# Key stage of a hybrid decoder step: triangles of two pairs inverted together, one running sum in place of two running products, affine steps moved or folded, low-rank products on whole rows

## The chip, the cores and the metric

The kernel runs on one core of a Trainium2 chip. The metric is the device time of one launch, in microseconds (us). Its engines are TensorE (PE in the rows, its weight loads PEld), VectorE (DVE), ScalarE (ACT), GpSimd (POOL) and SyncE (SP, which only issues transfers); each works through its own queue in order.

## The reference

One step of a decoder trunk of two layers: an RWKV-7 layer, then a latent attention layer, for a prompt of 1024 tokens and eight single tokens (the "sample"), in float32. The change lies in the first layer, in what stands ahead of its recurrence:

```python
def _wkv_step(S, inp):
    r, w, k, v, a, b = inp
    sa = jnp.einsum('bhvk,bhk->bhv', S, a)
    S = S * w[:, :, None, :] + sa[..., None] * b[:, :, None, :] + v[..., None] * k[:, :, None, :]
    return S, jnp.einsum('bhvk,bhk->bhv', S, r)
...
    w_log = -jax.nn.softplus(-(w0 + jnp.tanh(xw @ w1) @ w2)) - 0.5
    decay = jnp.exp(-jnp.exp(w_log.astype(F32)))
    a = jax.nn.sigmoid(a0 + (xa @ a1) @ a2)
    kk = heads(k * k_k).astype(F32)
    kk = kk / jnp.maximum(jnp.sqrt(jnp.sum(kk * kk, axis=-1, keepdims=True)), 1e-12)
    k = k * (1 + (a - 1) * k_a)
    xs = (seq(rh), seq(heads(decay)), seq(kh), seq(vh), seq(-kk), seq(kk * ah.astype(F32)))
```

## The kernel before, in words

The recurrence is done in 32 chunks of 32 tokens. What a chunk needs is made ahead, in the key stage, for 16 tiles of 128 channels (two heads each; `ct` is the tile). With `R` the receptance, `K` the key, `TW` and `TA` the hyperbolic tangents from the low-rank products of decay and rate, each tile does this, in the order of the loop over `ct`:

- `score` and `rows` of the tile before (`p`): TensorE forms the scores of a chunk in PSUM (`sc`), VectorE masks them to `XS`, ScalarE copies their triangles to `nts`, which SP stores to the scratch `n_d`; TensorE turns rows (`tr`), ScalarE copies them to `XS`, SP stores `xs_d`.
- `norm`: TensorE sums squares (`ss`), VectorE takes the maximum with a small number (`RN`), ScalarE a logarithm and an exponential of it (lines 784 and 785, a table load before each).
- `newkey`: VectorE makes `GG`, the new key, from `TA` and `K`, and an affine form of `TA`.
- `decay` (at the end of the tile before) and `decay2`: the decay's running product over a chunk, `Wp`, and its inverse, `Wi`, two scans on VectorE.
- `raw_rows`, `unit`, `unit2`, `unit_rows`: `RA` and `BK`, the operands of `score`, on VectorE; POOL multiplies `R` and `GG` into `K` (line 821), from which TensorE later adds up the bonus (`bo`).
- Beside this TensorE does the key projection of the next tile (`kproj`, product `p`, 24 steps a tile) and the two low-rank products (`ua`, product `u`), whose weights are cut in a high and a low part by `lora` and `lcut`.

Of every second tile on, POOL inverts the triangles of two pairs of heads (`inverse`, called by `whole`): (1 - N)^-1 of 128 triangles of 32 x 32, one a partition, in 31 steps, each a product into `Xt` and an addition to `X` (lines 1081 and 1083). Step s has (s+1) x (31-s) elements a partition. The triangles come back from `n_d` as `N`, and the result goes to `u_d`. The generator of the steps is `pend[0]`: `steps(g, n)` issues n steps of the projection and, after three of each four, one of the inverse. So the engines' queues are written by the order of the program: what POOL does for a tile stands behind the inverse steps that were issued before. The eighth inverse runs on VectorE at the end (`iv7`). The line that decides the pace:

```python
            def steps(g, n):
                for u in range(n):
                    next(g, None)
                    if u % 4 != 3:
                        next(pend[0], None)
```

A float32 product of the projections is made of three products of rounded parts (`mm3`, all on line 62). All pools give their buffers in turn, and an instruction waits for the reader of the buffer that it takes.

Of the kernel before, what the change touches and what calls it, by code (L numbers as in the profile page):

```python
# [11 lines left out]
F32 = mybir.dt.float32  # L12
F32R = mybir.dt.float32r
# [8 lines left out]
P = 128  # L22
# [22 lines left out]
# columns of the host-made constant table  # L45
# [10 lines left out]
def tile_yoco(ctx, tc, A, O, dbg=None):  # L56
    """A: name -> DRAM AP of the inputs, O: list of the ten DRAM outputs."""
# [36 lines left out]
    u_d = scr("u_d", (NC, 4, C, 6, C))  # L94
    u2_d = scr("u2_d", (NC, 2, 4, C, C))
# [2678 lines left out]
```

## Time and profile before

| | |
|---|---|
| time, median of 3 runs | 3003.13 us (2996.41 to 3007.01) |
| profiled execution, span | 3038.3 us, on the one core; granted TensorE clock 0.956 on the mean |
| TensorE busy | 2773.3 us, 91% of the span |
| VectorE, ScalarE, POOL busy | 1684.0, 1360.0, 1425.9 us |
| key stage, first `ss` of tile 0 to the last store of an inverse | 462.3 to 1004.2 us |

The span is that of the profiled execution, from its first to its last instruction; a time of its own beside the span is not given. Busy times are unions of an engine's instructions. An engine that is idle costs nothing by itself; what counts is which wait ends last.

### The profile page before, as it was taken

To read this page: it belongs to the slowest core of one execution; us is meant where nothing else is said; L and a number is where in the kernel's file an instruction comes from. 1 tells how busy PE (TensorE), PEld (TensorE's weight loads), DVE (VectorE), ACT (ScalarE), POOL (GpSimd) and SP (SyncE) were. 2 spreads that over 40 slices of the span, in tenths; PEclk is the share of its full clock that TensorE was granted. 3 is DMA by queue.
4 is the path that set the end of the run, shared out by engine and by line. 5 is a ranking of instruction groups with operands and counts; after the bars stand their busy time and mean duration, and the time that the engine had idled before them with its cause. 6 is when DMAs were issued, how large, how long until landed. Compare 5 with 4: busy or idle time off the path is not lost.

```text
span 3038.3 us, 64866 instructions
## 1 busy us (share of the span) xinstructions
PE 2773.3 (91%) x26386; PEld 2416.2 (80%) x26386; DVE 1684.0 (55%) x2952; ACT 1360.0 (45%) x2886; POOL 1425.9 (47%) x1385
## 2 busy tenths in 40 slices
PE   7999999878778788888789999999999999699998
PEld 7999997666567677777689899988888888465897
DVE  7233128979788466765752441176766666333424
ACT  7232127767656354445543452144444444233323
POOL 3222121899999366751354463123333332555342
PEclk9999999989889899999899999999999999899999
DMA  4332335667569899999675533231111111656535
GB/s 152 133 112 72 101 87 129 171 148 175 144 150 237 200 225 220 215 232 207 193 225 165 151 89 102 70 96 50 50 51 50 50 48 36 196 195 200 174 96 183
DMA packets 567501, 423.80 MB, mean 139 GB/s; under 512 B 176260, under 2 KB 515649, under 8 KB 567074
## 3 DMA queue, kind: packets, MB, share of 16 engines
q1 hardware_dynamic: 473954, 336.06, 41.2%
q10 hardware_dynamic: 79648, 38.42, 4.8%
q0 software_dynamic: 13600, 45.16, 4.7%
q8 instruction: 208, 3.41, 0.5%
q14 instruction: 91, 0.75, 0.1%
HBM read 281.69 MB, written 133.35 MB: 137 GB/s over the span
## 4 chain that ended last, share of the span: by engine, by line
PE 58%; DVE 7%; POOL 6%; DMA 5%; issue 4%; ACT 3%; SPq 1%; ACTq 0%; another core or an unknown queue 0%; DVEq 0%; POOLq 0%
PE sc L62 8%; PE p L62 7%; PE zb L62 6%; PE bo L62 5%; PE wop L62 4%; PE o L62 4%; POOL X L1083 2%; POOL Xt L1081 2%; PE q L62 2%; PE pt L2157 2%; PE s L62 2%; PE pt L2576 2%; PE k L62 2%; PE v L62 2%; PE ssc L62 1%
## 5 line engine op out<-in xcount | busy, mean ns | idle before, releaser
L76 POOL TENSOR_TENSOR wl<-wr,wh 128x1024 fp32r<-128x1024 f32 x32 | 84.2, 2653 | 287.5 <-ACT wh L71 269.8
L1081 POOL TENSOR_TENSOR Xt<-N,X 128x31 f32<-128x31 f32 (+15 forms) x217 | 188.7, 870 | 26.5 <-DMA N<-n_d 10.4
L1083 POOL TENSOR_TENSOR X<-X,Xt 128x31 f32<-128x31 f32 (+15 forms) x217 | 182.1, 839 | 17.0
L71 ACT CAST pth<-pt 128x256 fp32r<-128x256 f32 (+1 forms) x320 | 108.1, 354 | 139.8 <-DVE ptl L76 70.6
L1289 DVE TENSOR_TENSOR st<-s,gC 64x512 f32<-64x512 f32 x128 | 88.2, 689 | 130.0 <-PE s L62 127.5
L62 PE MATMUL p<-mh,w3h 128*128 128x344 f32 x384 | 149.1, 388 | 7.8 <-issue 6.6
L76 DVE TENSOR_TENSOR ptl<-pt,pth 128x256 fp32r<-128x256 f32 (+1 forms) x320 | 121.1, 392 | 29.1 <-ACT pth L71 27.0
L62 PE MATMUL p<-mh,w1h 128*128 128x344 f32 x360 | 136.0, 378 | 0.0
L62 PE MATMUL p<-ml,w3h 128*128 128x344 f32 x384 | 130.0, 339 | 2.2 <-DVE ml L76 2.2
L62 PE MATMUL p<-mh,w3l 128*128 128x344 f32 x384 | 126.8, 336 | 2.1 <-issue 2.1
L62 PE MATMUL r<-mh,wh 128*128 128x344 f32 x384 | 124.2, 323 | 3.3 <-ACT tf L483 3.1
L62 PE MATMUL r<-mh,wl 128*128 128x344 f32 x384 | 123.8, 323 | 0.0
L62 PE MATMUL r<-ml,wh 128*128 128x344 f32 x384 | 123.7, 322 | 0.0
L62 PE MATMUL p<-ml,w1h 128*128 128x344 f32 x360 | 120.7, 335 | 0.0
L62 PE MATMUL p<-mh,w1l 128*128 128x344 f32 x360 | 120.5, 335 | 0.0
L2509 POOL DMA_INDIRECT pg<-in_cache_ckv_dram,idx x64 | 60.6, 947 | 100.9 <-issue 50.8
L2140 ACT ACTIVATE pr<-sc,mx 128x128 f32<-128x128 f32 (+7 forms) x128 | 95.4, 745 | 26.7 <-DVE mx L2137 22.8
L2041 POOL TENSOR_TENSOR qp<-qp,rope 128x256 f32<-128x256 f32 (+1 forms) x30 | 22.2, 740 | 172.1 <-DMA qsw<-qp 167.3
L2137 DVE TENSOR_REDUCE mx<-sc 128x1 f32<-128x128 f32 (+7 forms) x128 | 96.8, 756 | 3.2
L1305 ACT COPY y<-y 32x256 f32<-32x256 f32 x256 | 93.0, 363 | 11.3 <-PE y L62 7.7
L62 PEld LDWEIGHTS s<-st,xz 128*64 128x64 f32 x2048 | 72.8, 148 | 30.1 <-issue 22.0
L1950 DVE TENSOR_TENSOR zbr<-zb,RS 128x384 f32<-128x384 f32 (+1 forms) x48 | 24.6, 515 | 127.4 <-PE zb L62 125.2
(1237 smaller groups left out, 9971.4 us busy)
## 6 DMA issues: line engine op xcount, KB each, us to landing
xs_d<-XS SPq DMA_DIRECT2D x64, 512.0 KB
xz<-xs_d SPq DMA_DIRECT2D x64, 512.0 KB
wr<-in_a_w_in_dram SPq DMA_DIRECT2D x17, 1024.0 KB
ra_d<-RA SPq DMA_DIRECT2D x32, 512.0 KB
xz<-ra_d ACTq DMA_DIRECT2D x58, 256.0 KB
rT_d<-rr ACTq DMA_DIRECT2D x16, 516.0 KB
R<-rT_d SPq DMA_DIRECT2D x16, 516.0 KB
w3r<-in_a_w_in_dram SPq DMA_DIRECT2D x16, 512.0 KB
```

What stands on the lines that cost most here:

```text
L62: PE.matmul(out, lhsT=lhsT, rhs=rhs, start=start, stop=stop)
L71: ACT.copy(out, in_)
L76: (eng or V).tensor_tensor(out, in_, hi_.bitcast(F32), ALU.subtract)
L1081: eng.tensor_tensor(t3, N_[:, s_:s_ + 1, s_ + 1:].to_broadcast([P, a, b]), X_[:, r0:r1, s_:s_ + 1].to_broadcast([P, a, b]), ALU.mult)
L1083: eng.tensor_tensor(X_[:, r0:r1, s_ + 1:], X_[:, r0:r1, s_ + 1:], t3, ALU.add)
L1289: V.tensor_tensor(ST[s_][1 - c % 2][rows, qs, :], p3[rows], gC[rows, qs, c:c + 1].to_broadcast([64, 8, 64]), ALU.mult)
L1305: ACT.copy(ys[B][ts(ci, 32), a:a + 2].rearrange("p a s d -> p (a s d)"), p_[ts(j, 32), 0:256])
L2137: V.tensor_reduce(mx, sc[:, :W], AX.X, ALU.max, negate=True)
L2140: ACT.activation(pr[:, :W], sc[:, :W], AF.Exp, bias=mx, accum_out=sm)
L2157: PE.transpose(pt[:, ts(q, P)], pr[:, ts(g + q, P)], ident)
L2509: G.indirect_dma_start(t_.rearrange("p r c -> p (r c)"), None, A[nm].rearrange("n (q r) c -> (n q) (r c)", r=4), off)
L2576: PE.transpose(p_[:, ts(r, P)], pg[:, r, ts(c, P)], ident)
```

## The change

It has four parts, all in the key stage.

1. `inverse` takes a list of one or two inverses and does their steps in the same instructions, over [128, 2, rows, columns]. `GROUPS` starts inverse 0 alone in tile 2, and the pairs 1 and 2, 3 and 4, 5 and 6 in tiles 6, 10 and 14. `pace` says after which of four projection steps an inverse step is issued: three of four for a single one and for the last pair, one of four for the others. Inverse 5 now goes to the second scratch `u2_d`, with 6 and 7.
2. The decay's running products become one running sum `CS` of `TW` + 1 (added on POOL), with one scan on VectorE whose factor `E0` (one byte) is zero at the head of a chunk. `Wp`, `Wi` and the chunk's end `gC` are then exponentials of it on ScalarE.
3. `GG`'s affine step goes to ScalarE. `TA`'s is folded into the products that read it.
4. The low-rank weights stand in both halves of the partitions, so that both products of `ua` and the cuts in `lcut` go over 128 rows. Some buffers have one copy in place of two.

```diff
             def lora(ct):
+                raw = kp.tile([P, 2, P], F32, tag="l2r", name=f"l2r{ct}")
+                for u in range(2):
+                    SY.dma_start(raw[ts(u, 64), 0], A["a_w2"][0][:, ts(ct, P)])
+                    SY.dma_start(raw[ts(u, 64), 1], A["a_a2"][0][:, ts(ct, P)])
...
-                        mm(p_[:, :NQ], d["l2"][me], th2[i][me, nsl[n]], False, True)
+                        mm(p_[:, :NQ], d["l2"][:, i], th2[i][:, nsl[n]], False, True)
...
             def decay(ct):
-                ACT.activation(Wp[:, :, 1:33], c3(TW), AF.Exp, bias=cneg, scale=-0.5 * CDEC)
-                ACT.activation(Wi[:, :, 1:33], c3(TW), AF.Exp, bias=cpos, scale=0.5 * CDEC)
+                G.tensor_scalar(CS[:, :, 1:33], c3(TW), 1.0, None, ALU.add)
...
             def decay2(ct):
-                for t_ in (Wp, Wi):
-                    V.memset(t_[:, :, 0:1], 0.0)
-                V.tensor_tensor_scan(fl(Wp), fl(Wp), fl(E0), 0.0, ALU.mult, ALU.add)
-                V.tensor_tensor_scan(fl(Wi), fl(Wi), fl(E0), 0.0, ALU.mult, ALU.add)
-                V.tensor_copy(gC[:, ct, :], Wp[:, :, 32])
+                V.tensor_tensor_scan(fl(CS), fl(E0), fl(CS), 0.0, ALU.mult, ALU.add)
+                ACT.activation(fl(Wp), fl(CS), AF.Exp, scale=-0.5 * CDEC)
+                ACT.activation(Wi, CS[:, :, 1:33], AF.Exp, scale=0.5 * CDEC)
+                ACT.activation(gC[:, ct, :], CS[:, :, 32], AF.Exp, scale=-0.5 * CDEC)
...
-                V.tensor_scalar(GG, TA, dv[:, 2, ct:ct + 1], dv[:, 3, ct:ct + 1], ALU.mult, ALU.add)
-                V.tensor_scalar(TA, TA, -0.5, -0.5, ALU.mult, ALU.add)
+                ACT.activation(GG, TA, AF.Identity, bias=dv[:, 3, ct:ct + 1], scale=dv[:, 2, ct:ct + 1])
...
-                V.tensor_tensor(d["TA"], d["TA"], d["RN"], ALU.mult)
+                V.scalar_tensor_tensor(d["TA"], d["TA"], 1.0, d["RN"], ALU.add, ALU.mult)
...
-                    if u % 4 != 3:
+                    if u % 4 in pace[0]:
                         next(pend[0], None)
...
+            GROUPS = {2: [0], 6: [1, 2], 10: [3, 4], 14: [5, 6]}
+            pace = [(0, 1, 2)]
+
+            def whole(qs):
+                n, q = len(qs), qs[0]
+                bufs = [ivp.tile([P, 2, C * C], F32, tag=t_, name=f"{t_}{q}")[:, 0:n] for t_ in "NX"]
+                pace[0] = (0, 1, 2) if n == 1 or q == 5 else (0,)
+                return inverse(qs, (*bufs, ivp.tile([P, C * C // 2], F32, tag="Xt", name=f"Xt{q}")), G, late)
...
         for s_ in range(C - 1):
+            a, b = s_ + 1, C - 1 - s_
+            t4 = tm[:, :n * a * b].rearrange("p (n a b) -> p n a b", n=n, b=b)
+            eng.tensor_tensor(t4, N_[:, :, s_:s_ + 1, s_ + 1:].to_broadcast([P, n, a, b]),
+                              X_[:, :, 0:a, s_:s_ + 1].to_broadcast([P, n, a, b]), ALU.mult)
+            eng.tensor_tensor(X_[:, :, 0:a, s_ + 1:], X_[:, :, 0:a, s_ + 1:], t4, ALU.add)
             yield
```

TensorE keeps its order. On POOL, in the changed kernel, this stands at the end of tile 6 and in tile 7 (the last of the first eight double steps, `CS` of tile 7, three double steps, and the product into tile 7's `K`; the numbers in the names tell buffers apart):

```order
L1081 TENSOR_TENSOR Xt_6229<-N_6227,X_6228 128x384
L1083 TENSOR_TENSOR X_6228<-X_6228,Xt_6229 128x2x8x24
L789 TENSOR_SCALAR CS<-TW_6271 128x32x32
L1081 TENSOR_TENSOR Xt_6229<-N_6227,X_6228 128x414
L1083 TENSOR_TENSOR X_6228<-X_6228,Xt_6229 128x2x9x23
L1081 TENSOR_TENSOR Xt_6229<-N_6227,X_6228 128x440
L1083 TENSOR_TENSOR X_6228<-X_6228,Xt_6229 128x2x10x22
L1081 TENSOR_TENSOR Xt_6229<-N_6227,X_6228 128x462
L1083 TENSOR_TENSOR X_6228<-X_6228,Xt_6229 128x2x11x21
L818 TENSOR_TENSOR K_6025<-R_6263,GG_6405 128x1024
```

Before, at the product into `K` of such a tile, POOL had this:

```order
L1081 TENSOR_TENSOR Xt_6338<-N_6336,X_6337 128x255
L1083 TENSOR_TENSOR X_6337<-X_6337,Xt_6338 128x17x15
L821 TENSOR_TENSOR K_6128<-R_6371,GG_6517 128x1024
L1081 TENSOR_TENSOR Xt_6338<-N_6336,X_6337 128x252
L1083 TENSOR_TENSOR X_6337<-X_6337,Xt_6338 128x18x14
```

A new instruction, `CS`, stands behind the steps of a tile; `K` stood behind 17 steps of its inverse there and stands behind three of the next tile's twelve now.

VectorE at the head of tile 7, before:

```order
L783 TENSOR_SCALAR RN_6505<-ss_2_6512 128x344
L806 TENSOR_SCALAR GG_6517<-TA_6380,dv 128x1032
L807 TENSOR_SCALAR TA_6380<-TA_6380 128x1032
L808 TENSOR_TENSOR GG_6517<-GG_6517,K_6128 128x1032
L796 MEMSET Wp 128x32
L796 MEMSET Wi 128x32
L797 SCALAR_TENSOR_TENSOR Wp<-Wp,E_4223 128x1056
L798 SCALAR_TENSOR_TENSOR Wi<-Wi,E_4223 128x1056
L799 COPY gC<-Wp 128x32
L813 TENSOR_TENSOR BK<-GG_6517,Wi 128x16x32
```

The same place of the changed kernel (the scans are printed as instructions of two tensors and a scalar):

```order
L782 TENSOR_SCALAR RN_6393<-ss_2_6400 128x344
L805 TENSOR_TENSOR GG_6405<-GG_6405,K_6025 128x1032
L794 SCALAR_TENSOR_TENSOR CS<-E_4224,CS 128x1056
L810 TENSOR_TENSOR BK<-GG_6405,Wi 128x16x32
```

Three instructions are left between `RN` and `BK` where there were nine, of which `GG` has an operand from ScalarE, the scan one from POOL and `BK` one from ScalarE.

ScalarE at the same place, of the changed kernel (before, `Wp` and `Wi` stood ahead of the logarithm, and the copies of `tr` came right behind the exponential of line 785):

```order
L783 ACT_TABLE_LOAD
L783 ACTIVATE RN_6393<-RN_6393 128x1032
L784 ACT_TABLE_LOAD
L784 ACTIVATE RN_6393<-RN_6393 128x1032
L804 ACTIVATE GG_6405<-TA_6272,dv 128x1032
L795 ACTIVATE Wp<-CS 128x1056
L796 ACTIVATE Wi<-CS 128x1024
L797 ACTIVATE gC<-CS 128x32
L870 COPY XS_0_6351<-tr_0_6433 64x4x64
```

`GG` has come in, and the two large exponentials and `gC` stand between it and the copies, behind VectorE's scan.

## Rows read from the trace of the kernel before

**Rows 1.** Windows by tiles: stretch, length, busy time (and count) of each engine, clock, DMA

```profile
core 0: us, PE busy (x) PEld busy (x) DVE busy (x) ACT busy (x) POOL busy (x), PEclk, DMA share, GB/s
462.30:512.80 50.50, 47.04 (x397) 38.44 (x396) 46.05 (x72) 38.41 (x72) 5.52 (x2) 0.94 0.44 108
512.80:563.10 50.30, 49.25 (x489) 40.17 (x485) 47.49 (x67) 42.54 (x87) 24.49 (x26) 1.00 0.77 187
563.10:626.00 62.90, 52.59 (x486) 42.53 (x484) 58.12 (x73) 43.01 (x87) 58.29 (x64) 0.89 0.65 155
626.00:756.90 130.90, 104.52 (x972) 84.92 (x968) 111.99 (x142) 86.24 (x173) 120.63 (x135) 0.90 0.67 158
756.90:886.40 129.50, 104.58 (x974) 85.02 (x969) 111.39 (x141) 86.07 (x173) 119.28 (x133) 0.89 0.67 157
886.40:927.80 41.40, 27.06 (x244) 22.05 (x242) 26.68 (x34) 21.23 (x42) 38.30 (x44) 0.79 0.55 138
```

**Rows 2.** Waits of TensorE, 462 to 928: sum, times, longest

```profile
PE bo L62 <- POOL K L821: 52.0, 9, 13.7
```

**Rows 3.** Timeline of POOL, tiles 3 to 5: start, length, instruction, idle before

```profile
540.54 0.24 POOL L1081 TENSOR_TENSOR Xt<-N,X 128x31 f32<-128x31 f32 x1 [9.26 <-DMA N<-n_d]
540.86 0.25 POOL L1083 TENSOR_TENSOR X<-X,Xt 128x31 f32<-128x31 f32 x1
...
544.33 2.41 POOL L1081 TENSOR_TENSOR Xt<-N,X 128x112 f32<-128x112 f32 x1
...
601.20 2.35 POOL L821 TENSOR_TENSOR K<-R,GG 128x1024 f32<-128x1024 f32 x1
...
605.17 0.65 POOL L1081 TENSOR_TENSOR Xt<-N,X 128x31 f32<-128x31 f32 x1
```

**Rows 4.** Timeline of POOL in the recurrence, two instructions of 512 elements

```profile
1040.23 1.04 POOL L1169 TENSOR_TENSOR tm<-sa,vs 128x512 f32<-128x512 f32 x1
1041.35 1.26 POOL L1171 TENSOR_TENSOR S<-S,tm 128x512 f32<-128x512 f32 x1
```

**Rows 5.** Timeline of VectorE, heads of tiles 1 and 2

```profile
490.96 0.81 DVE L806 TENSOR_SCALAR GG<-TA,dv 128x1032 f32<-128x1032 f32 x1
491.80 0.70 DVE L807 TENSOR_SCALAR TA<-TA 128x1032 f32<-128x1032 f32 x1
492.41 1.23 DVE L808 TENSOR_TENSOR GG<-GG,K 128x1032 f32<-128x1032 f32 x1
...
493.81 2.36 DVE L797 TENSOR_TENSOR_SCAN Wp<-Wp,E 128x1056 f32<-128x1056 f32 x1
...
498.52 0.69 DVE L813 TENSOR_TENSOR BK<-GG,Wi 128x512 f32<-128x512 f32 x1
...
518.92 2.36 DVE L797 TENSOR_TENSOR_SCAN Wp<-Wp,E 128x1056 f32<-128x1056 f32 x1
```

**Rows 6.** Timeline of ScalarE, head of tile 1: logarithm and exponential

```profile
491.49 1.07 ACT L784 ACTIVATE RN<-RN 128x1032 f32<-128x1032 f32 x1
...
493.87 1.07 ACT L785 ACTIVATE RN<-RN 128x1032 f32<-128x1032 f32 x1
```

**Rows 7.** Line 2049 on POOL, one input: least, median and greatest length in ns

```profile
L2049 POOL TENSOR_SCALAR qp<-qp x30: 847/849/1268, 1992.5 to 2537.5; 128x256 f32<-128x256 f32 x30
```

**Rows 8.** Groups by line, 455 to 970: busy, mean ns, idle before, releasers

```profile
L62 PEld LDWEIGHTS u<-th,l2l 64*128 64x128 f32 x96 | 18.2, 189 | 21.3 <-issue 21.0 <-DVE l2l L76 0.3
```

**Rows 9.** Chain of waits, tile 2: start, length, what

```profile
531.80 8.60 DMA N<-n_d
```

**Rows 10.** Timeline of POOL at the stage's end: stores of the last inverses

```profile
992.03 2.01 POOL L1091 DMA_DIRECT2D u_d<-X  x4 [0.29 <-POOL X L1083]
1002.71 1.93 POOL L1091 DMA_DIRECT2D u_d<-X  x4 [8.67 <-DVE X L1083]
```

**Rows 11.** Timeline of VectorE in the last inverse, two additions of 112 elements

```profile
975.21 0.73 DVE L1083 TENSOR_TENSOR X<-X,Xt 128x112 f32<-128x112 f32 x1
...
1000.56 0.27 DVE L1083 TENSOR_TENSOR X<-X,Xt 128x112 f32<-128x112 f32 x1
```

More of the change, by code (lines that the diff above doesn't have):

```diff
@@ L219, in phase_a @@
             omx = hp.tile([P, 48], F32, name="omx")
+            shT = hp.tile([P, KT, NB], F32, name="shT")
             w1x = px.enter_context(ExitStack())
@@ L619, in phase_a @@
             Wp = kp.tile([P, NC, 33], F32, name="Wp")
-            Wi = kp.tile([P, NC, 33], F32, name="Wi")
-            E0 = kp.tile([P, NC, 33], BF16, name="E0")
+            Wi = kp.tile([P, NC, 32], F32, name="Wi")
+            CS = kp.tile([P, NC, 33], F32, name="CS")
+            E0 = kp.tile([P, NC, 33], mybir.dt.uint8, name="E0")
             rkb = kp.tile([P, KI, H], F32, name="rkb")
@@ L670, in lcut @@
                 raw = st[ct]["l2r"]
-                s2 = st[ct]["s2"] = [kp.tile([P, P], F32R, tag=f"l2h{i}", name=f"l2h{i}_{ct}", bufs=2) for i in range(2)]
-                l2 = st[ct]["l2"] = kp.tile([P, P], F32R, tag="l2l", name=f"l2l{ct}", bufs=2)
-                for i in range(2):
-                    me = slice(64 * i, 64 * i + 64)
-                    hi(s2[i][0:64], raw[me])
-                    hi(s2[i][64:128], raw[me], V)
-                    lo(l2[me], raw[me], s2[i][me])
+                s2 = st[ct]["s2"] = kp.tile([P, 2, P], F32R, tag="l2h", name=f"l2h{ct}")
+                l2 = st[ct]["l2"] = kp.tile([P, 2, P], F32R, tag="l2l", name=f"l2l{ct}")
+                hi(s2, raw)
+                lo(l2, raw, s2)
             def rload(ct):
@@ L765, in evac @@
                         if ct == n == 0:
-                            zbank[1] = kp.tile([P, T], F32, tag="GG", name="zrow0", bufs=2)
+                            zbank[1] = kp.tile([P, T], F32, tag="GG", name="zrow0")
                         ACT.copy(zbank[1][:, nsl[n]], p_)
@@ L914, in phase_a @@
             zg = chain(*(zproj(ct, ct == 0) for ct in range(KI)))
-            def whole(q):
-                bufs = [ivp.tile([P, C * C], F32, tag=t_, name=f"{t_}{q}", bufs=b_) for t_, b_ in (("N", 2), ("X", 2))]
-                return inverse(q, (*bufs, [ivp.tile([P, C * C // 4], F32, tag="Xt", name=f"Xt{q}")]), [(G, 0, C)], late)
+            GROUPS = {2: [0], 6: [1, 2], 10: [3, 4], 14: [5, 6]}
[5 more added lines that the diff above has]
+                return inverse(qs, (*bufs, ivp.tile([P, C * C // 2], F32, tag="Xt", name=f"Xt{q}")), G, late)
             for ct in range(KI - 1):
@@ L953, in phase_a @@
                     rows(p, 3)
-                if ct % 2 == 0 and p >= 0:
+                if ct in GROUPS:
                     run(pend[0])
-                    fresh = whole(p // 2)
+                    fresh = whole(GROUPS[ct])
                     next(fresh)
@@ L971, in phase_a @@
                     mz_cut(1, G, G)
-                if ct % 2 == 0 and p >= 0:
+                if ct in GROUPS:
                     pend[0] = fresh
@@ L980, in phase_a @@
                 decay(ct + 1)
-                if ct == KI - 2:
-                    late.pop(0)()
+            assert not late
             p, ct = KI - 2, KI - 1
@@ L1021, in phase_a @@
             ra_store(ct, 0)
-            ivb.append([kp.tile([P, 16, C], F32, tag="nts", name="Xt7").rearrange("p a b -> p (a b)")])
-            iv7 = inverse(KI // 2 - 1, ivb, [(V, 0, C)], late)
+            ivb.append(kp.tile([P, 16, C], F32, tag="nts", name="Xt7").rearrange("p a b -> p (a b)"))
+            iv7 = inverse([KI // 2 - 1], ivb, V, late)
             next(iv7)
@@ L1037, in phase_a @@
             late[1]()
-            bT = kp.tile([H, T], F32, tag="GG", name="bT", bufs=2)
+            bT = kp.tile([H, T], F32, tag="TA", name="bT", bufs=2)
             for i in range(4):
```

67 lines of the change are left out of this document (29 added, 38 removed).

## The prediction

> **What bounds the kernel now.** I read the trace from the outside in. First the busy time of each engine between the first norm products (`ss`) of chosen tiles, which cuts the key stage into stretches that the changed kernel has too [rows 1]. Tiles 2 and 3 take 25.2 us each (50.30 / 2), with TensorE busy 24.6 us a tile, VectorE 23.7, ScalarE 21.3: nothing is spare and TensorE is the nearest to a bound. From tile 4 on it is another picture: 62.9 us for two tiles, 130.9 and 129.5 for four, 41.4 for the last, and in all of these POOL is busy more than nine tenths. Then the waits of TensorE: its longest sum is `bo` for POOL's `K` (line 821), 52.0 us [rows 2]. Then POOL's own rows in order of time [rows 3]: one inverse of a pair of heads starts at 540.54 and the next at 605.17, so POOL gives out one in 64.6 us, two tiles, and `K` stands in its queue between the steps. So POOL sets the pace of tiles 4 to 14, through the place of `K` in its queue, and the other engines set 25 us where POOL is free.
>
> **What a POOL instruction costs.** Alone, 31 elements take 0.24 us as a product and 0.25 as an addition [rows 3], 512 elements 1.04 and 1.26 [rows 4]; that is 0.19 us fixed, plus 1.66 ns and 2.10 ns an element, and about 0.08 between two. One inverse is 31 steps of (s+1)(31-s) elements, 5456 in all: 62 x 0.27 + 5456 x 3.76 ns = 37.2 us. With two `K` of 2.35 that makes 41.9; the period is 64.6. The other 22.7 us, 11 a tile, come from VectorE: a product of 112 elements, 0.38 by this rule, takes 2.41 us when it meets a scan [rows 3], 2.0 more.
>
> **The change part by part.**
> *Pairs.* 62 instructions of double size do two inverses: 62 x 0.27 + 10912 x 3.76 ns = 57.7 us instead of 74.4. Three times this saves 17 us of POOL, but see where the steps stand. A tile issues 20 steps of a single inverse, but 12 of a double one.
> *One scan.* VectorE loses 2.36 us and POOL some 2.0 us of obstruction a tile; two exponentials move behind the scan, `gC` moves to ScalarE. A scan over bytes instead of BF16 is not in the trace; the two scans there bound it (2.36 for the first, no reason for a gain).
> *Affine steps.* `GG` (0.81) and `TA` (0.70) leave VectorE [rows 5]; `GG` comes on ScalarE, 1.07 as the neighbours of the same 1032 elements [rows 6], and behind both of them. The -0.5 and the +1 go into instructions that exist; as three-operand forms I leave them at their old time. The +1 of the decay becomes a POOL instruction of 1024 elements (`CS`). Between 2.35 (`K`, same size, two inputs) and four times the one-input row of 256 elements, 0.849 [rows 7], less three fixed parts: 2.8. I take 2.8, the same operation. The Trainium skill, GPSIMD Engine Reference, section Engine selection, says that one-input work on GpSimd runs at roughly line rate; that would make `CS` an estimated 1.1 us and the total 14 us less. Rows 7 disagree: 0.849 for 256 elements is slower than a two-input sum of the slope above.
> *Whole rows.* The 96 half-height products leave; 21.0 us of idle time stood before their weights [rows 8]. It is TensorE time, some 1.3 us a tile or more, and TensorE stops being the bound below, so I count nothing; if ScalarE's chain were not there, it would be a gain of up to 20 us. Two more small loads a tile on SP lie ahead of `n_d` by a tile and cost nothing.
>
> **A tile without inverse steps.** At 491.49 ScalarE begins the logarithm, the exponential ends at 494.94 [rows 6]. Before, VectorE meanwhile did `GG`, `TA`, `GG*K` and began the first scan at 493.81, and `BK` came at 498.52 [rows 5]. Now: `GG` on ScalarE to 496.0, `GG*K` (1.23) to 497.3, the scan (2.36) to 499.6, `Wp` and `Wi` (1.07 each by their size) and `gC` to about 502: `BK` 3.3 us later. ScalarE's busy time of 21.3 gets 1.1 for `GG`, 0.2 for `gC`, less 0.2 for the merged casts, and it now stands still 3.6 us from 496.0 to 499.6 for VectorE, with about 1 us of its waits for TensorE left: 27 us a tile against 25.2. VectorE has 23.7 of work, less 3.9 and some small casts and copies, and waits for ScalarE before `GG*K` (some 4.7) and before `BK` (2.3): under 27, hidden behind ScalarE.
>
> **A tile with inverse steps.** `CS` of the next tile is issued at the end of a tile, so in POOL's queue it stands behind every step of that tile; VectorE's scan waits for it, and behind the scan on VectorE stand `BK`, `RA`, the score copies `XS` and everything else, behind `Wp` on ScalarE the transposed rows. Before, `K` stood half a tile ahead of its reader; `CS` has almost no lead. A tile is then POOL's sum from `CS` to `CS`, with VectorE's obstruction at 11 - 2.0 - 0.6 (affine, casts), say 8. A stretch is named by its tiles, from scan to scan, and set against rows 1.
> - 2 to 3: the load of `N` was issued 12.9 us after the scan (518.92 to 531.80) [rows 5, 9]; the rows that go ahead of it begin 3.5 later on ScalarE, of which I keep half, so 14.7. It lands 8.6 later [rows 9], at 23.3. Eight steps of 948 elements 7.9, obstruction 0.6, `CS` 2.9: 34.7.
> - 3 to 4: 20 steps, 4330 elements, 27.1; `K` 2.4, `CS` 2.9, 8: 40.4. Together 75.1 against 50.3: +24.8.
> - 4 to 6, three small steps only: 54 against 62.9: -8.9. 0 to 2: 54 against 50.5: +3.5.
> - 6 to 7: second load 1.8, so 25.1; eight double steps (1896) 11.4, 0.6, 2.9: 40.0. 7 to 8: twelve (5804) 28.3, 2.4, 2.9, 8: 41.6. 8 to 9: eleven (3212) 18.0, 2.4, 2.9, 8: 31.3; VectorE, held longer by longer POOL instructions, needs about 33, taken. 9 to 10: 27. Together 141.6 against 130.9 (+10.7) and against 129.5 for 10 to 14 (+12.1).
> - 14 to 15: 40 and 2.5 for the two cuts of mixed inputs that stand ahead on POOL: 42.5 against 41.4, +1.1.
> - Tail: 23 double steps are 46.3 alone instead of 29.4, +17; `K` of tile 15 no longer stands behind eight steps, -8; POOL had stored its part at 992.03 and been idle 8.67 before the last stores [rows 10], so alone it would just fit. But the last inverse is on VectorE, and beside POOL an addition of 112 elements takes 0.73, afterwards 0.27 [rows 11]: one instruction for each of POOL's. It began near 970, eight instructions before 975.21. With POOL's at 1.1 us on the mean and busy to about 1001 on the old scale, some 29 of the 62 are done by then, and 33 more of 0.2 to 0.43 take 11 us: 1012 against 1002.71. +9. By the Trainium skill, SBUF — State Buffer, section SBUF: two separate sides, the two engines' shared port pair is held by one for a whole instruction and the other fully blocks; the trace agrees in these two rows, and the rule speaks against longer POOL instructions.
>
> Sum: 3.5 + 24.8 - 8.9 + 10.7 + 12.1 + 1.1 + 9 = +52 us. The profiled span of 3038.3 would become 3090; it lies 35 us above the median of the runs shown, whose cause no row shows, and I carry the difference over unscaled: 3003 + 52 = 3055.
>
> **The rivals.**
> *Faster: POOL's total decides, not the order in its queue.* Four tiles then need 57.7 + 4 x 2.4 + 4 x 2.9 + 4 x 8 = 111 us of POOL instead of 130: -38 for both groups, -2 for the first six tiles, -13 for 14 to 15, +9 in the tail: -44, 2959. For it: POOL is the bound of before and its sum falls. Against: the place of `CS`. It decides where VectorE comes to its scan later than POOL to the end of `CS`, that is if VectorE's own tile is over 40 us. I give it and its halves 0.23.
> *No change.* `CS` 2.35 (-4), half the obstruction (-20), a free tile of 25 (-12), a tail of +2 (-7): +9. Small terms must all go one way: 0.09.
> *Slower still.* Instructions over four dimensions 20% dearer an element, which no row shows: +7 in each group, +7 in the tail, and VectorE held as much longer: 3077 to 3090. 0.13.
> The forecast, +15 to +75 by these pieces, has 0.55.
>
> **Numbers.** Within 0.3% (9 us) is about what a measurement of this kernel cannot tell from no change. Slower 0.68, same 0.09, faster 0.23. The range goes down into the halves of the faster rival, where a part of the waits is hidden, and up to the last rival: 2972 to 3088. The forecast's own range is 3018 to 3080.
>
> **What the changed profile would show.** VectorE's scan waits for POOL's `CS`, 10 us or more in tiles 3, 4, 7, 8, 11, 12 and 15; `bo` no longer waits for `K`. `GG*K` waits some 4 us for ScalarE in every tile, `BK` some 2. Tiles 4, 5, 9 and 13 take about 27 us with POOL mostly idle. POOL's largest steps take 1.0 to 1.3 us alone, `CS` near 2.8. The last inverse on VectorE ends later. I am wrong if the scan does not wait for `CS`, if `CS` is near 1 us, or if steps of 512 elements cost hardly more than those of 256.

## The result, and the profile after

The changed kernel takes 3071.7 us (median of 4 runs, 3067.43 to 3078.25), the kernel before on the same chip 3000.1 (4 runs, 2996.41 to 3007.01): ratio 1.0226, 95% interval 1.0201 to 1.0252, so 72 us slower where +52 were predicted. The profiled span is 3068.1 us. It lies only 30 above the span of the kernel before, because the two profiles come from different chips; in another stage, the sample attention (from the first to the last of its transpositions `pt`), one chip takes 206.3 us and the other 173.3 for the same work (see the end). The stages of the change are compared by themselves.

Windows of the changed kernel by tiles, each from the first scan of a tile to that of the next, columns as in [rows 1]: tiles 0 to 2, 2, 3, 4 to 6, then 6, 7, 8 and 9 singly, 10 to 14, 14, and the tail to the last store.

```profile
473.10:525.50 52.40, 42.91 (x423) 37.53 (x423) 36.67 (x52) 37.39 (x70) 12.47 (x4) 0.90 0.46 124
525.50:560.10 34.60, 26.81 (x290) 23.91 (x286) 17.96 (x27) 22.01 (x44) 13.54 (x21) 0.94 0.61 164
560.10:600.20 40.10, 26.77 (x242) 23.82 (x242) 24.47 (x26) 22.39 (x44) 37.12 (x44) 0.80 0.45 116
600.20:656.50 56.30, 45.86 (x442) 41.17 (x444) 37.11 (x52) 44.53 (x88) 14.99 (x11) 0.85 0.65 162
656.50:696.70 40.20, 27.16 (x292) 24.42 (x288) 18.24 (x28) 22.23 (x44) 18.06 (x21) 0.90 0.59 158
696.70:738.70 42.00, 27.15 (x242) 23.38 (x242) 29.70 (x26) 22.32 (x44) 38.58 (x27) 0.77 0.42 110
738.70:772.60 33.90, 22.03 (x160) 18.79 (x161) 26.57 (x27) 22.18 (x44) 27.87 (x24) 0.75 0.53 137
772.60:800.40 27.80, 26.05 (x286) 23.45 (x286) 18.48 (x28) 22.23 (x44) 5.44 (x2) 0.94 0.72 148
800.40:944.60 144.20, 100.78 (x976) 88.47 (x974) 92.59 (x106) 88.67 (x176) 90.08 (x72) 0.85 0.55 139
944.60:991.30 46.70, 23.42 (x246) 20.93 (x242) 22.73 (x27) 22.16 (x43) 25.92 (x24) 0.76 0.69 207
991.30:1073.30 82.00, 51.31 (x455) 44.56 (x455) 74.91 (x97) 38.73 (x78) 60.98 (x59) 0.77 0.71 179
```

From the first scan to the last lie 518.2 us, before 465.1: +53. From there to the last store 82.0, before 67.8: +14. Together +67 of the 72. In no stretch is an engine busy to the end: in tile 7 POOL is busy 38.6 of 42.0 us, but in tile 6 nobody is over 27.2 of 40.2. The time is in waits. These rows of the view show the largest ones of VectorE and some of ScalarE and TensorE (473 to 991 us: sum, times, longest):

```profile
DVE GG L805 <- ACT GG L804: 75.5, 16, 5.1
DVE CS L794 <- POOL CS L789: 49.4, 6, 12.6
DVE BK L810 <- ACT Wi L796: 29.3, 14, 2.1
ACT Wp L795 <- DVE CS L794: 108.3, 15, 16.9
PE tr L865 <- ACT XS L871: 102.0, 28, 16.4
PE ss L62 <- ACT nts L854: 26.2, 5, 7.0
```

They are one chain. VectorE's scan waits for POOL's `CS`, ScalarE's `Wp` for the scan, the copies `XS` stand behind `Wp` on ScalarE, and TensorE's transposed rows `tr` wait for their PSUM. TensorE's `bo` behind POOL's `K` [rows 2] is gone from the list.

The timeline of the changed kernel in tiles 6 to 8, and from tile 14 to the last store (start, length, instruction, idle before):

```profile
668.06 1.22 DVE L822 SCALAR_TENSOR_TENSOR TA<-TA,RN 128x1032 f32<-128x1032 f32 x1
669.80 0.68 DVE L827 SCALAR_TENSOR_TENSOR BK<-TA,Wi 128x512 f32<-128x512 f32 x1
669.96 1.44 ACT L692 ACTIVATE TW<-u,dv 128x344 f32<-128x344 f32 x3
671.65 3.69 SPq L1074 DMA_DIRECT2D N<-n_d  x2
681.81 0.29 POOL L1081 TENSOR_TENSOR Xt<-N,X 128x62 f32<-128x62 f32 x1 [12.19 <-DMA N<-n_d]
692.89 0.98 POOL L1083 TENSOR_TENSOR X<-X,Xt 128x384 f32<-128x384 f32 x1
693.85 2.77 POOL L789 TENSOR_SCALAR CS<-TW 128x1024 f32<-128x1024 f32 x1
696.65 3.05 DVE L794 TENSOR_TENSOR_SCAN CS<-E,CS 128x1056 f32<-128x1056 uint8 x1 [12.09 <-POOL CS L789]
699.74 1.08 ACT L795 ACTIVATE Wp<-CS 128x1056 f32<-128x1056 f32 x1 [16.56 <-DVE CS L794]
707.23 2.64 POOL L818 TENSOR_TENSOR K<-R,GG 128x1024 f32<-128x1024 f32 x1 [1.69 <-DVE RN L816]
707.56 3.41 DVE L822 SCALAR_TENSOR_TENSOR TA<-TA,RN 128x1032 f32<-128x1032 f32 x1
712.35 1.71 DVE L827 SCALAR_TENSOR_TENSOR BK<-TA,Wi 128x512 f32<-128x512 f32 x1
723.96 1.34 POOL L1083 TENSOR_TENSOR X<-X,Xt 128x512 f32<-128x512 f32 x1
738.72 3.17 DVE L794 TENSOR_TENSOR_SCAN CS<-E,CS 128x1056 f32<-128x1056 uint8 x1 [5.00 <-POOL CS L789]
...
953.23 0.62 ACT L71 CAST w3h<-w3r 128x512 fp32r<-128x512 f32 x1 [4.09 <-DMA w3r<-in_a_w_in_dram]
966.99 2.27 SPq L1074 DMA_DIRECT2D N<-n_d  x2
976.49 0.29 POOL L1081 TENSOR_TENSOR Xt<-N,X 128x62 f32<-128x62 f32 x1 [5.54 <-DMA N<-n_d]
1032.17 1.09 DVE L1081 TENSOR_TENSOR Xt<-N,X 128x31 f32<-128x31 f32 x1
1039.59 1.08 DVE L1083 TENSOR_TENSOR X<-X,Xt 128x112 f32<-128x112 f32 x1
1057.80 0.42 POOL L1083 TENSOR_TENSOR X<-X,Xt 128x62 f32<-128x62 f32 x1
1069.26 0.27 DVE L1083 TENSOR_TENSOR X<-X,Xt 128x112 f32<-128x112 f32 x1
1071.39 1.93 POOL L1092 DMA_DIRECT2D u_d<-X  x4 [8.92 <-DVE X L1083]
```

What the reader is to see in tile 6: the triangles are there at 681.81, 25.3 us after the scan; eight double steps follow back to back, and `CS` behind them, although its input `TW` is done at 671.4. VectorE stands still 12.1 us for it and ScalarE 16.6.

### The profile page after: what moved, and what is told of

Its sections match the earlier page's. It is cut to its first block, busy times and chain, and to the rows that moved or that the text cites. A ratio compares the mean times of both kernels' runs of the same rounds, so it can differ in the third digit from the quotient of the medians.

```text
span 3068.1 us, 64652 instructions
## 1 busy us (share of the span) xinstructions
PE 2744.9 (89%) x26386; PEld 2428.7 (79%) x26386; DVE 1618.3 (53%) x2808; ACT 1372.5 (45%) x2902; POOL 1345.3 (44%) x1214
## 3 DMA queue, kind: packets, MB, share of 16 engines
q1 hardware_dynamic: 476450, 336.59, 40.1%
q8 instruction: 208, 3.41, 0.5%
## 4 chain that ended last, share of the span: by engine, by line
PE 52%; DVE 5%; DMA 5%; issue 3%; ACT 2%; POOL 1%; SPq 0%; ACTq 0%; DVEq 0%; POOLq 0%
PE sc L62 7%; PE zb L62 6%; PE bo L62 4%; PE p L62 4%; PE wop L62 4%; PE o L62 3%; PE q L62 2%; PE pt L2158 2%; PE k L62 2%; PE s L62 2%; PE v L62 2%; PE pt L2577 2%; PE ssc L62 1%; PE bt L62 1%; PE qp L62 1%
## 5 line engine op out<-in xcount | busy, mean ns | idle before, releaser
L865 PE MATMUL tr<-ctab,BK 128*128 128x128 f32 x256 | 50.1, 344 | 119.8 <-ACT XS L871 119.8
L865 PEld LDWEIGHTS tr<-ctab,BK 128*128 128x128 f32 x256 | 37.1, 174 | 130.0 <-ACT XS L871 129.2
L1081 POOL TENSOR_TENSOR Xt<-N,X 128x120 f32<-128x120 f32 (+23 forms) x124 | 112.9, 911 | 50.4 <-DMA N<-n_d 42.0
L1083 POOL TENSOR_TENSOR X<-X,Xt 128x120 f32<-128x120 f32 (+23 forms) x124 | 126.7, 1022 | 9.7
L818 POOL TENSOR_TENSOR K<-R,GG 128x1024 f32<-128x1024 f32 x16 | 40.4, 2527 | 170.8 <-DVE RN L816 132.6
L2141 ACT ACTIVATE pr<-sc,mx 128x128 f32<-128x128 f32 (+7 forms) x128 | 95.4, 745 | 27.8 <-DVE mx L2138 26.4
```

The lines of the kernel that those rows point to most:

```text
L818: G.tensor_tensor(d["K"][:, :S], d["R"][:, :S], d["GG"][:, :S], ALU.mult)
L865: PE.transpose(p_[:, ts(m, P)], BK[:, 8 * g + 2 * m:8 * g + 2 * m + 2, :], ident)
L1081: eng.tensor_tensor(t4, N_[:, :, s_:s_ + 1, s_ + 1:].to_broadcast([P, n, a, b]), X_[:, :, 0:a, s_:s_ + 1].to_broadcast([P, n, a, b]), ALU. ...
L1083: eng.tensor_tensor(X_[:, :, 0:a, s_ + 1:], X_[:, :, 0:a, s_ + 1:], t4, ALU.add)
L2141: ACT.activation(pr[:, :W], sc[:, :W], AF.Exp, bias=mx, accum_out=sm)
```

## The experiments

Theory: `CS` at its place in POOL's queue and `GG` on ScalarE turn into waits of VectorE, and cost more than the pairs, the one scan and the whole rows can give back. Rivals: the double instructions themselves are what costs, or the uneven spread of their steps over the tiles. In the table "tiles" is first scan to last scan, "tail" from there to the last store, both in the profile of that run; the ratio is to the kernel before on the same chip. A difference between two runs is that of their ratios, times 3000 us; by the intervals it is good to 8 to 13 us.

| kernel | tiles, us | tail, us | ratio, 95% interval |
|---|---|---|---|
| before | 465.1 | 67.8 | 1 |
| changed | 518.2 | 82.0 | 1.0226 (1.0201 to 1.0252) |
| +1 on VectorE | 471.5 | 84.0 | 1.0086 (1.0065 to 1.0107) |
| `GG` on VectorE | 495.9 | 82.2 | 1.0142 (1.0123 to 1.0161) |
| single inverses | 541.6 | 66.6 | 1.0262 (1.0236 to 1.0287) |
| steps spread evenly | 528.9 | 82.1 | 1.0280 (1.0249 to 1.0312) |
| half rows again | 531.7 | 82.4 | 1.0290 (1.0266 to 1.0314) |
| both on VectorE | 430.4 | 85.4 | 0.9949 (0.9930 to 0.9968) |
| both, spread evenly | 425.7 | 95.8 | 0.9963 (0.9942 to 0.9985) |
| both, last inverse alone | 439.6 | 77.8 | 0.9947 (0.9929 to 0.9966) |
| both, single inverses | 431.4 | 73.6 | 0.9911 (0.9877 to 0.9945) |
| the same, `K` on VectorE | 400.2 | 79.9 | 0.9849 (0.9821 to 0.9876) |
| before with whole rows | 462.7 | 67.8 | 1.0012 (0.9996 to 1.0028) |
| the same, with pairs | 450.5 | 86.2 | 1.0016 (0.9996 to 1.0036) |

**The two moved steps, one at a time and together.**

```diff
-                G.tensor_scalar(CS[:, :, 1:33], c3(TW), 1.0, None, ALU.add)
+                V.tensor_scalar(CS[:, :, 1:33], c3(TW), 1.0, None, ALU.add)
```

> One edit to the changed kernel: the +1 that makes CS is added on VectorE instead of POOL, so nothing of POOL's stands ahead of the scan. Queue theory (the scan waits for CS, which stands behind the inverse steps): the scan-to-scan times of tiles 3, 7, 8, 11, 12 fall from 34 to 42 us towards 28 to 31, 14 to 15 from 46.7 to about 29; K falls behind on POOL by less than its slack, so TensorE's wait for K stays below 15 us in all. About 84 us less than the changed kernel, near 2988. Rival (POOL's sum decides, wherever CS stands): only the time of CS itself goes, 2.8 us in eight bound tiles, near 3050. Rival (ScalarE's longer chain is the cost): no change beyond 10 us.

Measured: 1.0086, 42 us faster than the changed kernel (0.0140 x 3000), half of the 84 expected; the tiles lose 47, the tail gains 2. The wait of the scan is gone, but tiles without inverse steps stay at 28 us, and tiles 7 and 8 take 36.5 and 38.9 where 28 to 31 were expected. The windows of tiles 8 and 9 show why:

```profile
707.60:746.50 38.90, 27.43 (x256) 23.53 (x256) 31.58 (x29) 22.47 (x44) 36.86 (x29) 0.82 0.46 119
746.50:775.30 28.80, 25.31 (x288) 22.59 (x284) 18.40 (x29) 22.26 (x44) 6.28 (x6) 0.94 0.71 149
```

VectorE takes 31.6 us for its 29 instructions beside POOL's double steps, and 18.4 for 29 where POOL has little to do. With 7.3 us of waits, for `GG` and `Wi` from ScalarE and for TensorE, that is the whole of tile 8: behind the wait for `CS` stood a second bound, VectorE held by POOL.

```diff
-                ACT.activation(GG, TA, AF.Identity, bias=dv[:, 3, ct:ct + 1], scale=dv[:, 2, ct:ct + 1])
+                V.tensor_scalar(GG, TA, dv[:, 2, ct:ct + 1], dv[:, 3, ct:ct + 1], ALU.mult, ALU.add)
```

> One edit to the changed kernel: the affine step of GG is back on VectorE. Chain theory: the wait of GG*K for ScalarE (70.9 us in 15 tiles) goes, and the seven tiles without inverse steps fall from about 28 to 24.5 us, while the tiles that wait for CS keep their time: 20 to 25 less, near 3048. Rival (the wait for GG lies beside the wait for CS or for TensorE and costs nothing): no change, 3072. Rival (VectorE is as good as full): slower by 0.8 us in 16 tiles, 3085.

Measured: 1.0142, 25 us faster. Free tiles fall from 27.2 to 28.8 us to 22.8 (24.4 in tile 4). Tiles 3, 6, 7, 10 and 11 stay at 40 to 43, tile 14 grows from 46.7 to 51.0, and the scan waits longer for `CS`, 86.5 us in all against 58.2. `GG` is the price of the free tiles, `CS` that of the loaded ones.

Both edits together:

> Both edits together: the +1 of CS and the affine step of GG on VectorE, pairs, one scan, folded steps and whole rows kept. Theory (the two waits that the change makes, for CS and for GG, are the loss; one scan, whole rows and pairs are gains): tiles without POOL work at 23 us, the loaded ones at 32 to 36 since double instructions hold VectorE, the key stage to the last scan near 405 us against 465 before, the tail still 84 against 68: about 45 us below the kernel before, ratio 0.985. Rival (the waits were beside each other, so that taking both away gives no more than the better one): ratio 1.005 to 1.01.

Measured: 0.9949, 83 us faster than the changed kernel and 15 faster than before; the single moves give 42 + 25 = 67, so each hid a part of the other. The rival fell, but the 45 us below the kernel before were not reached: the tiles take 430.4 and not 405, tile 8 still 39.1. Some of the wait of before comes back, as the waits (462 to 940 us) of this run show; with `GG` in one buffer VectorE waits for POOL's `K` as well as `bo`:

```profile
PE bo L62 <- POOL K L818: 16.8, 4, 6.9
DVE GG L804 <- POOL K L818: 14.5, 4, 6.3
```

No run gave `GG` its second buffer back by itself.

**The pairs.** Here `GROUPS` is that of single inverses, with two buffers of `N` and `X`; the store of the seventh stands at the end of tile 14.

```diff
-            GROUPS = {2: [0], 6: [1, 2], 10: [3, 4], 14: [5, 6]}
+            GROUPS = {2 * i + 2: [i] for i in range(7)}
...
-                bufs = [ivp.tile([P, 2, C * C], F32, tag=t_, name=f"{t_}{q}")[:, 0:n] for t_ in "NX"]
+                bufs = [ivp.tile([P, 1, C * C], F32, tag=t_, name=f"{t_}{q}", bufs=2) for t_ in "NX"]
```

> The pairing undone: seven single inverses on POOL, one every second tile, issued as before the change; all else of the changed kernel kept. Queue theory: CS then stands behind eight steps after the triangles' arrival in even tiles (35 us from scan to scan) and behind twenty steps in odd ones (40), 75 for two tiles against 72 with pairs: 20 to 30 more until tile 14, 10 to 20 less in the last tile and the tail, 3080 within 15. Rival (the long double instructions are the cost, since they hold VectorE): faster by 20 or more, below 3050.

Measured: 1.0262, 11 us slower than with pairs, which is at the edge of what the intervals tell apart. In the profile tiles alternate between 35 and 40 us, 23 us more in all; the tail is that of before again, 15 us less. So the pairs do help the tiles while the scan waits for `CS`, and take most of it back at the end.

The same edit, with both steps on VectorE:

> The changed kernel with the decay's +1 and GG's affine step both on VectorE and the inverses single again, as in the kernel before; the one running sum and the whole rows stay. It asks what the pairs are worth once the two waits are gone (with pairs the scans lay 430 us apart from first to last, the tail after the last scan was 85 us, the ratio 0.995). Theory (a double instruction saves POOL a fixed part, but holds VectorE longer and ends the last inverse later): tiles without inverse steps 23 us, the loaded tiles all about 30, scan sum about 440 and tail about 67, so some 8 us faster than with pairs, ratio 0.988 to 0.993. Rival (the saved fixed parts, 17 us in all, are worth their time): slower than with pairs, ratio 0.998 to 1.002, scan sum near 455.

Measured: 0.9911, 11 us faster than with pairs, again at the edge of the intervals. The tiles are the same (431.4 and 430.4), the tail is 12 shorter. With the two waits gone the fixed parts that the pairs save are worth nothing in the tiles, and the gain of the single inverses lies in the tail alone. (By the prediction's sum a pair saves 17 us, so the three save 50, and not 17 in all.) Free tiles before the first inverse take 23.2, as expected; the loaded ones 33 and 27 in turn, 30 on the mean. The waits (462 to 940 us) name POOL's `K`:

```profile
PE bo L62 <- POOL K L818: 50.2, 11, 6.9
DVE GG L804 <- POOL K L818: 43.9, 11, 6.3
```

Whether `K` is late for its place in the queue or because POOL has too much to do, they do not tell.

The last run on this question puts the pairs into the kernel before, with its own products and affine steps (and the whole rows). `E0` is a byte a number instead of two there, to make room.

```diff
-                V.tensor_tensor_scan(fl(CS), fl(E0), fl(CS), 0.0, ALU.mult, ALU.add)
-                ACT.activation(fl(Wp), fl(CS), AF.Exp, scale=-0.5 * CDEC)
...
+                V.tensor_tensor_scan(fl(Wp), fl(Wp), fl(E0), 0.0, ALU.mult, ALU.add)
+                V.tensor_tensor_scan(fl(Wi), fl(Wi), fl(E0), 0.0, ALU.mult, ALU.add)
```

> The kernel before with the pairs of inverses (and the whole rows, which alone gave a ratio of 1.001), but with its own two running products and all affine steps where they were. Theory (the pairs do no harm by themselves; it was CS in POOL's queue that turned them into waits): K of tiles 7 and 8 stands behind 11 and 12 double steps and has half a tile of lead, so a group of four tiles takes 106 to 115 us instead of 130, tiles 4 to 6 some 10 less, the tail 10 to 14 more: ratio 0.985 to 0.99. Rival (double instructions hold VectorE and end the last inverse later, as between the runs with both steps on VectorE, where pairs cost 11 us): ratio 1.0 to 1.006, tiles loaded with double steps 35 us or more and VectorE's largest instructions 3 us and longer.

Measured: 1.0016, no change. The rival's ratio held, though of the loaded tiles 7 to 9 only tile 8 takes the 35 us that it names. The tiles win 12 us against whole rows alone, where the theory's pieces make 40 to 58: tiles 6 to 9 take 24.6, 31.4, 38.1 and 33.3 us, 127.4 together and not 106 to 115, and `bo` still waits 47.6 us for `K`. The tail gives back 18.

**The spread of the double steps.** Eight steps beside the single projection steps at a tile's end, none between; and the store of a finished pair moves to the tile in which the next one begins.

```diff
-                pace[0] = (0, 1, 2) if n == 1 or q == 5 else (0,)
+                pace[0] = (0, 1, 2) if n == 1 or q == 5 else ()
...
+                    while late:
+                        late.pop(0)()
...
                     steps(kpr, 1)
+                    if not pace[0]:
+                        next(pend[0], None)
```

> The changed kernel with the double steps dealt out evenly: eight a tile over four tiles in place of 8, 12 and 11 over three (a finished pair is stored when the next begins). Queue theory: CS to CS becomes 40, 32, 32 and 27 in place of 40, 42, 34 and 28, about 13 less in each of two groups and none in the last: about 25 us below the changed kernel, ratio to the kernel before near 1.015. Rival (POOL's sum decides): no change, 1.023.

Measured: 1.0280, 16 us slower, where a gain was expected. The windows of tiles 6 to 9:

```profile
659.90:699.70 39.80, 26.80 (x289) 24.06 (x284) 18.11 (x27) 22.11 (x44) 17.98 (x20) 0.89 0.61 162
699.70:735.50 35.80, 23.42 (x177) 20.01 (x179) 26.34 (x27) 22.30 (x44) 26.17 (x18) 0.74 0.50 129
735.50:771.10 35.60, 26.77 (x232) 23.24 (x229) 26.83 (x27) 22.54 (x44) 26.01 (x18) 0.81 0.51 130
771.10:802.20 31.10, 26.62 (x296) 23.68 (x296) 22.46 (x26) 22.24 (x44) 17.41 (x16) 0.95 0.58 149
```

Together 142.3 us, against 143.9; the work was only dealt out. A tile with eight double steps takes 36 us and not the 32 expected. Tiles 10 and 14 take 45.9 and 52.1, 5 us more each. Two rows of POOL, from tile 7 and tile 10, show the causes:

```profile
708.09 2.38 POOL L818 TENSOR_TENSOR K<-R,GG 128x1024 f32<-128x1024 f32 x1 [8.42 <-DVE RN L816]
829.50 1.80 POOL L1079 MEMSET X<- 128x2048 f32 x1 [16.49 <-DMA u_d<-X]
```

With no steps left between `CS` and `K`, POOL stands still 8.4 us until VectorE has made `RN`. And the store of the finished pair, now issued in tile 10, holds the buffer that POOL has to clear for the next one. Neither forecast held for the whole kernel; that tiles 6 to 9 keep their sum is what the rival says. The place of the store was not undone by itself.

The same edit, with both steps on VectorE:

> The two edits and the even dealing of the double steps. Theory (a tile lasts as long as POOL's share of steps, and VectorE's hold, in it): 23, 29, 29 and 25 in place of 23, 32, 36 and 23 in each group, some 8 us less per group than with both edits alone, ratio 0.98. Rival (the hold of VectorE is the same wherever the steps stand): the same as with both edits alone.

Measured: 0.9963 against 0.9949, the same within the intervals: the tiles win 5 us and the tail loses 10. The forecast of 8 us less in each group fell: the two groups take 122.2 and 128.0 us, with both edits alone 119.6 and 121.6. Only the last tile is shorter, by 13.7, and the tail takes most of that back.

With the pairs two tiles earlier, both steps on VectorE (the quick pace goes to the pair 4 and 5, and a finished pair is stored when the next begins):

```diff
-            GROUPS = {2: [0], 6: [1, 2], 10: [3, 4], 14: [5, 6]}
+            GROUPS = {4: [0, 1], 8: [2, 3], 12: [4, 5], 14: [6]}
```

> The two edits, and the pairs moved: 0 and 1 from tile 4, 2 and 3 from tile 8, 4 and 5 from tile 12, and 6 alone from tile 14. Theory of the tail (23 double steps on POOL hold the last inverse on VectorE): the tail from the last scan to the last store falls from 84 to about 68, as before the change; tiles 12 to 14 get slower, 75 us for two, so that the whole is within 10 us of both edits alone, ratio 0.98 to 0.99. Rival (the tail is long for another cause, such as eight more stores on POOL's queue): the tail stays above 80.

Measured: 0.9947, no different. The tail is 8 us shorter, but at 77.8 it lies between the 68 of the theory and the 80 of the rival; tile 13 takes 45.8. So the double steps are a part of the long tail, and the rest of it stays open.

**The whole rows.** The half-height form of before (`lora`, `lcut` and the two products of `ua`) in the changed kernel:

```diff
-                        mm(p_[:, :NQ], d["l2"][:, i], th2[i][:, nsl[n]], False, True)
+                        mm(p_[:, :NQ], d["l2"][me], th2[i][me, nsl[n]], False, True)
```

> The low-rank weights as before the change, on half of the partitions each, all else of the changed kernel kept. Theory (TensorE is not the bound in the key stage now): TensorE's idle time before those 96 products comes back, about 20 to 36 us of its own time, and does not show; two more casts and one more subtraction on VectorE cost at most 1 us in the seven free tiles: 3072 to 3080. Rival (whole rows shorten the path): 3092 or more.

Measured: 1.0290, 19 us slower than with whole rows; the theory fell, and the rival's 3092 was missed by about a microsecond. Tiles without steps take 30 to 32 us, those that `CS` sets stay at 40 and 41. The waits of ScalarE (473 to 1006 us) in this run:

```profile
ACT TA L695 <- PE u L62: 17.7, 28, 0.6
ACT TW L695 <- PE u L62: 16.7, 27, 2.0
```

In the changed kernel the same two are 1.2 and 2.8 us. Where ScalarE's chain sets a free tile, half a microsecond that each low-rank product is late counts. Not all of the 19 us is TensorE's: ScalarE is busy 22.9 us in tile 1 against 22.0, with more and smaller casts.

The other way round, `lora`, `lcut` and `ua` of the change in the kernel before:

```diff
-                        mm(p_[:, :NQ], d["l2"][me], th2[i][me, nsl[n]], False, True)
+                        mm(p_[:, :NQ], d["l2"][:, i], th2[i][:, nsl[n]], False, True)
```

> The kernel before with the whole-row low-rank products alone: both halves of the partitions loaded, cut and multiplied, and nothing else of the change. Theory (POOL sets tiles 4 to 14 of the kernel before, so TensorE's saved time counts in the first four tiles alone): some 1 us a tile there, 4 us in all, ratio 0.997 to 1.0. Rival (the 20 us that these rows were worth in the changed kernel are TensorE's and are gained here too): 15 to 20 us, ratio 0.993 to 0.995, the scan sum 445 to 450 for 465.

Measured: 1.0012, no change. In the kernel before, tiles 4 to 14 hang on POOL, and the wait of TensorE only grows (waits, 462 to 940 us; before 52.0 [rows 2]):

```profile
PE bo L62 <- POOL K L818: 87.3, 6, 15.5
```

The first tiles do win: 23.1 and 23.2 us for tiles 1 and 2, before 25.1 and 25.3.

This run (1.0012) and the one with both steps on VectorE and single inverses (0.9911) were timed on the same chip, and differ in the key stage by the one running sum, the folded step of `TA` and the single buffer of `GG`. Between them lie 30 us, 31 in the tiles: this part of the change, which no run took apart further, is the one that gains.

**`K` off POOL.** Single inverses, both steps on VectorE, and the product for the bonus too:

```diff
-                G.tensor_tensor(d["K"][:, :S], d["R"][:, :S], d["GG"][:, :S], ALU.mult)
+                V.tensor_tensor(d["K"][:, :S], d["R"][:, :S], d["GG"][:, :S], ALU.mult)
```

> As the run with single inverses and both affine steps on VectorE, and the product of R and GG into K moved from POOL to VectorE too. Theory (the place of K in POOL's queue, behind the inverse steps, sets the loaded tiles, as it did in the kernel before): no wait of bo for POOL is left, a loaded tile goes from about 30 to 28 us, scan sum 15 to 25 us shorter, ratio some 0.006 lower. Rival (POOL's total with VectorE's obstruction sets the loaded tiles, or VectorE becomes the bound): scan sum within 8 us of the run without this edit.

Measured: 0.9849, 45 us faster than before and 113 faster than the changed kernel: the fastest here. Loaded tiles go from 33 and 27 in turn to some 25 and 29, the tiles lose 31 us. `bo` waits no more; the longest wait of TensorE (462 to 940 us) is now one for ScalarE:

```profile
PE ss L62 <- ACT nts L854: 30.4, 13, 4.7
```

The forecast held, but the run does not tell the place of `K` from POOL's sum, because it also takes the product of 2.4 us off POOL in each tile. Two loaded tiles of the run without this edit, and two of this one:

```profile
sum 60.50, PE 48.22 PEld 43.18 DVE 46.55 ACT 41.79 POOL 55.66; mean PE 24.11 PEld 21.59 DVE 23.28 ACT 20.89 POOL 27.83
sum 53.80, PE 46.08 PEld 39.68 DVE 48.81 ACT 41.99 POOL 49.43; mean PE 23.04 PEld 19.84 DVE 24.40 ACT 21.00 POOL 24.72
```

POOL is busy 92% of both pairs of tiles; it loses 6.2 us and the tiles lose 6.7. The rival's 8 us left out that the edit shortens POOL.

Only the last tile goes the other way, 38.6 us for 28.3: VectorE waits 11.5 us there in one piece for a weight of the gate, `w3h`, which ScalarE cuts late because it waits 8.6 us for the load of `w3r`.

## Why the prediction was right, and where its sizes were off

**The mechanism was right; the margin of the waits was not.** The stretches, predicted and measured: tiles 0 to 2 54 and 52.4; tile 2 34.7 and 34.6; tile 3 40.4 and 40.1; 4 to 6 54 and 56.3; tiles 6 to 9 40.0, 41.6, 33, 27 and 40.2, 42.0, 33.9, 27.8. `CS` costs 2.77 us (2.8 taken). The estimate of 1.1 from the Trainium skill (GPSIMD Engine Reference, section Engine selection: one-input work at roughly line rate) is 1.7 us short for this instruction; here the measurement decides. `GG` times `K` waits 75.5 / 16 = 4.7 us for ScalarE, as worked out, `BK` 2.1 (2.3). The triangles of tile 6 are there after 25.3 us (25.1). The runs that take one edit back confirm both places: `GG` sets the free tiles, `CS` the loaded ones, and with both undone the ratio is 0.9949 (0.9930 to 0.9968). The sign rests on these two.

The waits of the scan were foretold at 10 us or more in seven tiles. They are 7.1, 7.6, 12.1, 5.0, 12.6, 5.0 and 8.8. In tiles 7 and 8 VectorE comes late itself, with `TA` at 3.41 us beside POOL's `K` (1.22 in tile 6) and `BK` at 1.71 beside its steps (0.68 in tile 6, with POOL idle). With `CS` off POOL's queue tile 8 still takes 38.9 us. So the condition of the faster rival, a tile of VectorE of over 40 us, failed by little: POOL's sum did give tiles 3, 6 and 7 to half a microsecond, but VectorE's own time was closer to that sum than I saw.

**The terms that were mis-sized.** The difference is 72 us where 52 were predicted. The stage explains 15 of these 20: tiles 0 to 6 nothing (-1.6, -0.1, -0.3, +2.3), the groups of four tiles 2.3 and 2.6, tile 14 4.2, the tail 5. The other 5 are within the interval of the ratio (60 to 75 us).
- *Tile 14.* I counted the load of `N` as in tile 6 and 2.5 for the cuts. But SP issues it at 966.99, 22.4 us after the scan, where it is 15.1 in tile 6 (671.65). ScalarE stands still 4.1 us there for the load of a weight of the gate (953.23), so the copies `XS`, whose store goes ahead of `N` on SP, begin 9.3 us after the scan and not 4.6; and a load of the mixed inputs (1.8 us) stands between the stores. The first step comes 31.9 us after the scan, not 27.6. That is the 4.2.
- *The tail.* The last inverse was predicted to end late for POOL's double steps, with 29 of its 62 instructions done when POOL ends and 33 left. In the trace POOL's last step ends at 1058.2, the 29th instruction 0.3 us later, and the 33 left end 12.9 us after POOL; an addition of 112 elements takes 1.08 us beside POOL and 0.27 alone [rows 11]. What was missed: POOL ends 66.9 us after the scan, not 64.2, and the rest takes 12.9 and not 11. That the count of 29 is met is luck: the inverse begins 40.9 us after the scan and not some 33 as before, and beside POOL its instructions follow each other every 0.9 us and not every 1.1. The Trainium skill (SBUF — State Buffer, section SBUF: two separate sides) says that the port pair which the two engines share belongs to one of them for a whole instruction; the trace agrees, since VectorE's addition of 112 elements lasts 1.08 us where POOL's double step beside it takes 1.03.
- *Free tiles.* 27 taken, 27.2 to 28.9 measured.

**Where I was wrong without a price.** The whole rows were counted as nothing, with "a gain of up to 20 us if ScalarE's chain were not there". The condition was the wrong way round: with ScalarE's chain they are worth 19 us, mostly because the late products delay its tangents; in the kernel before, where POOL sets the pace, nothing. The 27 us of a free tile already left ScalarE only about 1 us of waits for TensorE, and it is the whole rows that bring this about.

**The rivals.** "POOL's total decides" (2959) did not come about, and even without `CS` in the queue the pairs gave nothing: in the kernel before with whole rows they changed the time by 0.0004 of it. What a shorter POOL gains in the tiles (12 us there), the tail takes back (18), where longer instructions hold VectorE. The rival of dearer four-dimensional instructions fell by its rows: the steps of 384 elements take 0.85 and 0.98 us, the rule gives 0.83 and 1.00.

What stays open: why the tail is 6 us longer than before (73.6 and 67.8) with both steps on VectorE and single inverses; what a second buffer of `GG` would give; and an earlier load of the gate's weight in tile 14, for which ScalarE waits 4.1 us in the changed kernel and 8.6 in the fastest one: no run tried it.

## What to carry to other kernels

An instruction moved to an idle engine costs what stands ahead of it in that engine's queue: ask where in the order it is issued and who reads it next, before its length. A value with half a tile of lead may stand behind a few steps (`K` behind three double ones: no wait of `bo`), but not behind seventeen single ones (52.0 us before), and one that is read at once behind none (`CS`): 42 us here for some 0.7 us of VectorE's time a tile. Longer instructions save an engine its fixed part, but hold its neighbour longer; look at what runs beside them at the end of the stage.

## What was not expected of the hardware

- The same sample attention takes 173.0 to 174.7 us on the chips where the kernel before takes 3000 to 3004 us, and 202 to 209 where it takes 3037 to 3039, with the same gathers. The transfers of that stretch, kernel before on one chip (2605 to 2820 us):

```profile
DMA packets 12788, 42.64 MB, mean 198 GB/s; under 512 B 2223, under 2 KB 2351, under 8 KB 12768
```

and the changed kernel on another (2670 to 2850 us):

```profile
DMA packets 12547, 41.96 MB, mean 233 GB/s; under 512 B 2194, under 2 KB 2322, under 8 KB 12529
```

These 33 us are nearly all of the 35 between the profiled span of before and its median, which no row of that profile alone could explain; why the gathers run slower on some chips is open. Ratios are to the kernel before on the same chip for this reason.
- An addition of a constant to 1024 numbers takes POOL 2.78 us, the product of two tensors of that size 2.38 (medians of 16, changed kernel): one input is not cheaper. VectorE does the same addition in 0.68 to 1.52 us, 0.69 on the median, in the run with the +1 on VectorE.
